# The opening of a hybrid conv/mLSTM block on one Trainium2 core: p in halves of positions, a constant's zeros to warm TensorE, low parts on GpSimd, x loaded and turned in another order

## Chip, core and metric

One core of a Trainium2 chip runs the whole kernel as one launch. The metric is the device time in microseconds (us), as a median over runs. The engines are called by the profile's names: PE is the matrix engine and PEld its weight loads, DVE is VectorE, ACT is ScalarE, POOL is GpSimd, SP is the engine that issues most DMAs. L545 is line 545 of the kernel before.

## The reference, cut to what matters

x is 512 positions by 1024, p is 512 by 256, all in float32.

```python
hn   = rmsnorm(x, g_mix)
proj = hn @ w_in                  # (512, 1024) @ (1024, 14344), split into xa, ba, ..., q, k, v, o, zb, gates
...                               # short convolution, chunked mLSTM, gated merge
x = x + merged @ w_o
gate = sigmoid(rmsnorm(x, g_ple) @ w_ple_gate)
x = x + gate * (p @ w_ple)        # (512, 256) @ (256, 1024): this product is made first, in the opening
return rmsnorm(x, g_final)
```

## The kernel before, in words

Every float32 product is made of three products of a faster format: an operand u is split into a high part `hi` (a copy by ACT that rounds to fp32r) and a low part `lo = u - hi` (a subtraction), and `mm3` (L231 to L235) adds hi·hi, hi·lo and lo·hi into one PSUM bank. Weights come in chunks of 512 rows by 512 columns into four buffers `wraw`; `split_half` (L178) makes the two parts of half a chunk, the high one on ACT (L180) and the low one on DVE, or on POOL if it is told so (L181).

PE, ACT, DVE and POOL run their instructions in the order in which the code states them. SP issues DMAs in the order of the code too; each waits until the transfer that last used one of eight completion semaphores has landed. After the opening the code is a long chain of matmul blocks (plain ones, `block_fm` and `block_tm`, and Strassen products), and the splits of coming weights and the work on results are handed out between the matmul groups by `tick`.

The change lies in the opening, L472 to L640, which does two things before the first block of x @ w_in:

- `ple = p @ w_ple`. p is loaded as `pin` in four tiles of 128 positions (t = 0 to 3), turned by PE into PSUM (`turn_p`, L531, one bank for each half k of the 256 rows), and split into `pT[0]` and `pT[1]`. `w_ple` comes as four quarters (2n + k: n is the half of the 1024 columns, k the half of the 256 rows) into `raws[0]` and is split into `whi[q]` and `wlo[q]`. Each of the eight results (n, t) takes 2 × 3 matmuls of 512 columns; `keep_ple` copies a finished bank out of PSUM, on ACT or, if told so, on DVE (L559), and the copies are stored to DRAM.
- The norm of x. For each tile t: `square_x` on ACT (L535) gives the sum of squares, `power_x` is one small DVE instruction (L538) and a power -0.5 on POOL (L539), `scale_x` is two small DVE instructions (L543, L544) and one over the tile (L545). The first small one needs the power from POOL. `turn_x(k)` (L550) turns column block k of all four tiles and cuts it into `hn_hi` (ACT) and `hn_lo` (DVE) with the gain `gm`, a slice of `prm`, which is `prow` turned by PE (L628) and copied by DVE (L629).

PE's order there: seven matmuls on a zeroed `hn_lo` (`keep_warm`, L491: six at the start, one after the second half of p is turned), the turns of p, the 24 matmuls of n = 0, 21 of the 24 of n = 1, the turn of `prow`, `turn_x(0)` to `turn_x(2)`, the last three matmuls of `ple`, `turn_x(3)`. Then the block on chunk 1 begins, first with the half whose parts `split_half(1, 0)` makes (low part on POOL), and `turn_x(4)` to `turn_x(7)` stand between its groups of six matmuls.

DVE's order for x: `power_x(0)`, a copy of a PSUM bank, `power_x(1)`, the low parts of quarters 2 and 3, `scale_x(0)`, `scale_x(1)`, `power_x(2)`, `power_x(3)`, `scale_x(2)`, `scale_x(3)`, the copy of `prm`, then the low parts of `turn_x`.

POOL's order: small constants, five loads of parameters into `prow` (L512 to L516), the loads of `wg_raw` and `bg` (L517, L518), a memset of `wg` (L526), the four powers, the low parts of chunk 1 (L181).

SP's order: `pin` tiles 0 and 1, quarters 0 and 1 of `w_ple`, x tiles 0 and 1, quarters 2 and 3, x tiles 2 and 3, then the chunks of w_in (L148). ACT issues `pin` tiles 2 and 3.

Of the kernel before, what the change touches and what calls it, by code (L numbers as in the profile page):

```python
# [20 lines left out]
NH = 4  # L21
# [15 lines left out]
def hybrid_block(ctx, tc, x, p, g_mix, w_in, conv_w, conv_b, w_a_out, b_gates, g_head,  # L37
                 w_b_out, w_o, g_ple, w_ple_gate, w_ple, g_final, out):
    nc = tc.nc
    act, dve, pool, pe = nc.scalar, nc.vector, nc.gpsimd, nc.tensor  # L40
# [7 lines left out]
    ps_x = ctx.enter_context(tc.tile_pool(name="ps_x", bufs=4, space=bass.MemoryType.PSUM))  # L48
# [13 lines left out]
    w_in_v = w_in[0].rearrange("(kt p) n -> p kt n", p=P)  # L62
# [6 lines left out]
    chunks, operands = [], []  # L69
    H2 = S // 2  # L70
# [69 lines left out]
    state = {"raw": 0, "split": 0, "use": 0}  # L140
    raws, splits, pieces, active, fresh = {}, {}, deque(), [], []

    def load_raw(between=None):
        i = state["raw"]
        state["raw"] += 1
        raws[i] = spare[i] if i in spare else wraw.tile([P, HC, CW], F32, name=f"wraw{i}", tag="wraw")
        for src, ks, cs in chunks[i]:
            nc.sync.dma_start(raws[i][:, ks, cs], src)  # L148
# [82 lines left out]
    def mm3(ps, a, b, first, last, **kw):  # L231

        pe.matmul(ps, lhsT=a[0], rhs=b[0], start=first, stop=False, **kw)  # L233
        pe.matmul(ps, lhsT=a[0], rhs=b[1], start=False, stop=False, **kw)  # L234
        pe.matmul(ps, lhsT=a[1], rhs=b[0], start=False, stop=last, **kw)  # L235
# [17 lines left out]
    ident = const.tile([P, P], F32, name="ident")  # L253
# [20 lines left out]
    hn_hi = hnp.tile([P, KT, S], F32R, name="hn_hi", align_bytes=256)  # L274
# [14 lines left out]
    def bank(m, tag=None):  # L289
        return ps_mm.tile([P, S], F32, name="mm", tag=tag or order[m // 2], bufs=2)  # L290
# [193 lines left out]
    load_ple(0)

    dve.memset(hn_lo[:, 0, :].bitcast(F32), 0.0)
    warm = bank(2)

    def keep_warm(n):
        for _ in range(n):  # L490
            pe.matmul(warm, lhsT=hn_lo[:, 0, :P], rhs=hn_lo[:, 0, :], start=True, stop=True)  # L491
# [20 lines left out]
    nc.gpsimd.dma_start(prow[0:8, :], g_mix[0].rearrange("(c p) -> c p", p=P))  # L512
# [4 lines left out]
    nc.gpsimd.dma_start(wg_raw, w_in_v[:, :, IG:IG + 2 * NH])  # L517
# [8 lines left out]
    pool.memset(wg.bitcast(F32), 0.0)  # L526

    def turn_p(k):
        pt = bank(k)
        for t in range(NT):  # L530
            pe.transpose(pt[:, t * P:(t + 1) * P], pin[:, t, k * P:(k + 1) * P], ident)  # L531
        return pt

    def square_x(t):
        act.activation(sq, xin[:, t, :], AF.Square, accum_out=ss[:, t:t + 1])  # L535

    def power_x(t):
        dve.tensor_scalar(tmp[0][:, t:t + 1], ss[:, t:t + 1], 1.0 / D, EPS, ALU.mult, ALU.add)  # L538
        pool.tensor_tensor(tmp[1][:, t:t + 1], tmp[0][:, t:t + 1], mhalf[:, :1], ALU.pow)  # L539

    def scale_x(t):
        a, r, e = (u[:, t:t + 1] for u in tmp)
        dve.scalar_tensor_tensor(e, r, a, r, ALU.mult, ALU.mult)  # L543
        dve.tensor_scalar(e, e, -0.5, 1.5, ALU.mult, ALU.add)  # L544
        dve.tensor_scalar(xin[:, t, :], xin[:, t, :], r, e, ALU.mult, ALU.mult)  # L545

    def turn_x(k):
        pt = ps_x.tile([P, S], F32, name="pt", tag="x")
        for t in range(NT):
            pe.transpose(pt[:, t * P:(t + 1) * P], xin[:, t, k * P:(k + 1) * P], ident)  # L550
        cut(hn_hi[:, k, :], hn_lo[:, k, :], pt, gm[:, k:k + 1])
# [4 lines left out]
    def keep_ple(t, n, ps, on_dve=False):  # L556
        u = ples[4 * n + t]
        if on_dve:
            dve.tensor_copy(u, ps)  # L559
        else:  # L560
            act.activation(u, ps, AF.Copy)
# [21 lines left out]
    act.activation(hi, raw, AF.Copy)
# [11 lines left out]
    whi, wlo = ([splits[0][q // HH][u][:, q % HH, :] for q in range(4)] for u in range(2))
    state["use"] = 1
    splits.pop(0)

    def ple_part(ps, n, k, t):
        mm3(ps, [u[:, k, t * P:(t + 1) * P] for u in pT], [whi[2 * n + k], wlo[2 * n + k]], k == 0, k == 1)  # L600

    pss = [ps_x.tile([P, S], F32, name="mmp", tag="x") for t in range(NT)]
    for i, (a, b) in enumerate(((pT[0], whi), (pT[1], whi), (pT[0], wlo))):
        for t in range(NT):
            pe.matmul(pss[t], lhsT=a[:, 0, t * P:(t + 1) * P], rhs=b[0], start=i == 0, stop=False)
# [18 lines left out]
    pss = [bank(t) for t in range(NT)]
    for k, t in [(0, 0), (0, 1), (0, 2), (0, 3), (1, 0), (1, 1), (1, 2)]:
        ple_part(pss[t], 1, k, t)
    pt = ps_x.tile([P, S], F32, name="pt", tag="x")
    pe.transpose(pt[:, :64], prow, ident[:64, :64])  # L628
    dve.tensor_copy(prm, pt[:, :64])  # L629
    for t in range(2):  # L630
        keep_ple(t, 1, pss[t])

    split_half(1, 0, pool)
    for k in range(3):
        turn_x(k)
    ple_part(pss[3], 1, 1, 3)
    for t in range(2, NT):
        keep_ple(t, 1, pss[t])
# [875 lines left out]
```

## Time and profile before

| | |
|---|---|
| median of 3 runs | 838.82 us (838.82 to 839.24) |
| the profiled execution | 839.31 us; its span in the trace 837.2 us |
| PE busy | 826.9 us, 99% of the span, 4520 matmuls |
| DVE, ACT, POOL busy | 680.7, 526.0, 212.8 us |
| DMA | 170.73 MB, mean 204 GB/s |
| granted PE clock | 0.998 on the mean |

A timeline row gives the start in the span, the busy time, the engine, line and operation, what is written and read, and in brackets how long the engine had been idle and for whom it waited. A row of the chain of work gives start, duration and the instruction that was the last thing waited for. Consecutive instructions of one kind are merged into one row (x8).

### The profile page before, as it was taken

The page shows a single profiled execution, that of the slowest core. Times are in us where ns is not written, and L with a number is a line of the kernel's source. Part 1 is how long each engine was busy: PE and PEld are TensorE (multiplying, and loading weights), DVE is VectorE, ACT ScalarE, POOL GpSimd, SP SyncE. Part 2 cuts the span into 40 slices and gives each one's busy share as a digit, 9 for nine tenths or more (in the row PEclk, how much of TensorE's full clock was granted, in tenths as well). Part 3 has the DMA queues.
Part 4 walks back from the last instruction along what each step waited for, and adds up shares of the span by engine and source line. Part 5 has one row for each costly group of instructions (what it writes and reads, how often), then busy time and mean ns, then how long its engine had stood idle before and what let it go on. Part 6 is the DMA issues. An engine that isn't in the chain of part 4 may idle for free.

```text
span 837.2 us, 12110 instructions
## 1 busy us (share of the span) xinstructions
PE 826.9 (99%) x4520; PEld 720.6 (86%) x4520; DVE 680.7 (81%) x938; ACT 526.0 (63%) x778; POOL 212.8 (25%) x213
## 2 busy tenths in 40 slices
PE   9999999999999999999999999999999999999996
PEld 7888888878889988888888999999998888888885
DVE  5788768898888777789978999797985778999565
ACT  7467665788765776667876485545447365657553
POOL 5203122213124221220222334342411212131031
PEclk9999999999999999999999999999999999999999
DMA  9748789759969896985998789999989488999402
GB/s 318 264 150 182 152 220 225 202 182 274 212 149 187 217 240 168 259 215 147 264 225 199 152 179 235 181 182 182 183 268 377 96 191 224 276 260 239 178 1 100
DMA packets 102626, 170.73 MB, mean 204 GB/s; under 512 B 5600, under 2 KB 47124, under 8 KB 101800
## 3 DMA queue, kind: packets, MB, share of 16 engines
q0 software_dynamic: 39136, 69.28, 43.7%
q1 hardware_dynamic: 59792, 94.64, 34.5%
q10 hardware_dynamic: 3640, 6.04, 2.2%
q8 instruction: 35, 0.57, 0.3%
q14 instruction: 23, 0.19, 0.1%
HBM read 153.16 MB, written 16.79 MB: 203 GB/s over the span
## 4 chain that ended last, share of the span: by engine, by line
PE 94%; DVE 2%; DMA 1%; issue 1%; ACT 1%; POOL 0%; POOLq 0%; ACTq 0%
PE mm L233 29%; PE mm L234 29%; PE mm L235 29%; DMA wraw<-in_w_in 1%; PE pv L235 1%; PE pv L233 1%; PE pv L234 1%; PE sc L235 1%; PE sc L234 1%; PE sc L233 1%; PE ptk L1307 0%; PE pth L1188 0%; PE pt L550 0%; PE mm L491 0%; DVE xin L545 0%
## 5 line engine op out<-in xcount | busy, mean ns | idle before, releaser
L181 DVE TENSOR_TENSOR wlo<-wraw,whi 128x1024 fp32r<-128x1024 f32 x244 | 299.5, 1228 | 83.0 <-ACT whi L180 76.3
L180 ACT ACTIVATE whi<-wraw 128x1024 fp32r<-128x1024 f32 x246 | 257.9, 1054 | 85.4 <-PE mm L235 36.1
L156 POOL DMA_DIRECT2D wraw<-in_w_in x106 | 129.3, 1395 | 294.7 <-DVE wlo L181 200.1
L346 ACT ACTIVATE s<-mm 128x512 f32<-128x512 f32 x84 | 50.2, 598 | 83.4 <-PE mm L235 82.2
L233 PE MATMUL mm<-whi,hs 128*128 128x512 f32 x256 | 99.8, 390 | 0.4 <-DVE c L350 0.4
L234 PE MATMUL mm<-wlo,hs 128*128 128x512 f32 x256 | 99.9, 390 | 0.2 <-DVE wlo L181 0.2
L235 PE MATMUL mm<-whi,hs 128*128 128x512 f32 x256 | 99.7, 389 | 0.0
L233 PE MATMUL mm<-hn_hi,whi 128*128 128x256 f32 (+1 forms) x304 | 93.3, 307 | 0.0
L235 PE MATMUL mm<-hn_hi,wlo 128*128 128x256 f32 (+1 forms) x304 | 93.1, 306 | 0.0
L234 PE MATMUL mm<-hn_lo,whi 128*128 128x256 f32 (+1 forms) x304 | 92.9, 305 | 0.0
L233 PE MATMUL mm<-hs,whi 128*128 128x256 f32 x320 | 90.6, 283 | 0.0
L234 PE MATMUL mm<-hs,whi 128*128 128x256 f32 x320 | 90.6, 283 | 0.0
L235 PE MATMUL mm<-hs,wlo 128*128 128x256 f32 x320 | 90.6, 283 | 0.0
L233 PE MATMUL mm<-whi,hn_hi 128*128 128x512 f32 x192 | 74.7, 389 | 0.0
L234 PE MATMUL mm<-wlo,hn_hi 128*128 128x512 f32 x192 | 74.7, 389 | 0.0
L235 PE MATMUL mm<-whi,hn_lo 128*128 128x512 f32 x192 | 74.7, 389 | 0.0
L233 PEld LDWEIGHTS mm<-hs,whi 128*128 128x128 f32 x320 | 61.4, 192 | 0.0
L234 PEld LDWEIGHTS mm<-hs,whi 128*128 128x128 f32 x320 | 61.4, 192 | 0.0
L235 PEld LDWEIGHTS mm<-hs,wlo 128*128 128x128 f32 x320 | 61.4, 192 | 0.0
L235 PEld LDWEIGHTS mm<-hn_hi,wlo 128*128 128x128 f32 x304 | 58.1, 191 | 2.9 <-POOL wlo L181 0.3
L234 PEld LDWEIGHTS mm<-hn_lo,whi 128*128 128x128 f32 x304 | 58.1, 191 | 2.4
L233 PEld LDWEIGHTS mm<-hn_hi,whi 128*128 128x128 f32 x304 | 58.1, 191 | 2.4
(345 smaller groups left out, 1728.1 us busy)
## 6 DMA issues: line engine op xcount, KB each, us to landing
wraw<-in_w_in SPq DMA_DIRECT2D x32, 1024.0 KB, 5.3
wraw<-in_w_in SPq DMA_DIRECT2D x48, 512.0 KB, 4.9
wraw<-in_w_in POOLq DMA_DIRECT2D x46, 512.0 KB, 7.6
wraw<-in_w_in POOLq DMA_DIRECT2D x60, 256.0 KB, 5.8
wraw<-in_w_b_out SPq DMA_DIRECT2D x7, 1024.0 KB, 6.9
wraw<-in_w_b_out POOLq DMA_DIRECT2D x12, 512.0 KB, 6.8
wraw<-in_w_o SPq DMA_DIRECT2D x5, 1024.0 KB, 6.9
wraw<-in_w_a_out SPq DMA_DIRECT2D x4, 1024.0 KB, 5.1
```

The costliest lines, as they stand in the source:

```text
L156: nc.gpsimd.dma_start(raws[to][:, ks, cs], src[:, ks, :], accum_op=ALU.add)
L180: act.activation(hi, t, AF.Copy)
L181: (e_lo or dve).tensor_tensor(lo, t, hi.bitcast(F32), ALU.subtract)
L233: pe.matmul(ps, lhsT=a[0], rhs=b[0], start=first, stop=False, **kw)
L234: pe.matmul(ps, lhsT=a[0], rhs=b[1], start=False, stop=False, **kw)
L235: pe.matmul(ps, lhsT=a[1], rhs=b[0], start=False, stop=last, **kw)
L346: act.activation(to[i], src, AF.Copy, scale=scale)
```

## The change

- Loads. Quarter 0 of `w_ple` goes first, on ACT's queue. SP then takes `pin` tiles 0 and 1, `pin` tiles 2 and 3, quarter 1, x tiles 0 and 1, quarter 2, x tiles 2 and 3, quarter 3. Each chunk-1 load is cut in two (256 KB pieces, both column pieces of the first 256 rows before those of the second).
- PE is warmed by eight matmuls of 128 columns on a constant's zeros; the memset of `hn_lo` and the seventh warming matmul are gone.
- p is turned, copied and split in halves of positions (256 columns of a bank at a time); the first matmuls run on tiles 0 and 1 while tiles 2 and 3 are still to be turned.
- The low parts of all four quarters of `w_ple` are subtracted by POOL. The high part of quarter 3 is made by DVE. `wg`'s memset moves to the front of POOL's loads, and the loads of `wg_raw` and `bg` behind the low parts of quarters 0 and 1.
- x is turned by halves: tiles 0 and 1 for column blocks 0 to 3, then tiles 2 and 3. `power_x(3)` stands behind `scale_x(2)` and the copy of `prm`, and the low part of quarter 3 (POOL) between that power and `scale_x(3)`.

```diff
     qk_block(1)
+    chunks[1] = [(src[:, k:k + HH], slice(k, k + HH), cs) for k in (0, HH) for src, _, cs in chunks[1]]
     qk_block(0)
...
-    for i, queue in enumerate((nc.sync, nc.scalar)):
-        queue.dma_start(pin[:, 2 * i:2 * i + 2, :], p_v[:, 2 * i:2 * i + 2, :])
-    def load_ple(n):
-        for src, ks, cs in chunks[0][2 * n:2 * n + 2]:
-            nc.sync.dma_start(raws[0][:, ks, cs], src)
-    load_ple(0)
-    dve.memset(hn_lo[:, 0, :].bitcast(F32), 0.0)
+    def load_ple(q, queue=nc.sync):
+        src, ks, cs = chunks[0][q]
+        queue.dma_start(raws[0][:, ks, cs], src)
+    load_ple(0, nc.scalar)
+    for i in range(2):
+        nc.sync.dma_start(pin[:, 2 * i:2 * i + 2, :], p_v[:, 2 * i:2 * i + 2, :])
+    load_ple(1)
     warm = bank(2)
-    def keep_warm(n):
-        for _ in range(n):
-            pe.matmul(warm, lhsT=hn_lo[:, 0, :P], rhs=hn_lo[:, 0, :], start=True, stop=True)
-    keep_warm(6)
+    zeros = nc.const_aps.tensor(0.0, [P, P], F32)
+    for _ in range(8):
+        pe.matmul(warm[:, :P], lhsT=zeros, rhs=zeros, start=True, stop=True)
...
-    for i in range(2):
-        for t in range(2 * i, 2 * i + 2):
-            nc.sync.dma_start(xin[:, t, :], x_v[:, t, :])
-        if i == 0:
-            load_ple(1)
+    for t in range(NT):
+        nc.sync.dma_start(xin[:, t, :], x_v[:, t, :])
+        if t % 2:
+            load_ple(2 + t // 2)
     load_raw()
+    pool.memset(wg.bitcast(F32), 0.0)
...
-    nc.gpsimd.dma_start(wg_raw, w_in_v[:, :, IG:IG + 2 * NH])
-    nc.gpsimd.dma_start(bg, b_gates[0].rearrange("(g h) -> h g", g=2))
-    pool.memset(wg.bitcast(F32), 0.0)
...
-    ptp = turn_p(0)
-    dve.tensor_copy(pT[0][:, 0, :], ptp)
...
-    low(pT[0][:, 0, :], pT[1][:, 0, :], ptp)
-    low(hi, lo, raw)
-    ptp = turn_p(1)
-    keep_warm(1)
-    split_quarter(1, dve)
-    cut(pT[0][:, 1, :], pT[1][:, 1, :], ptp)
...
-    power_x(0)
-    keep_ple(0, 0, pss[0], True)
-    power_x(1)
-    for hi, lo, raw in quarters:
-        act.activation(hi, raw, AF.Copy)
-        low(hi, lo, raw)
-    keep_ple(1, 0, pss[1])
-    scale_x(0)
-    scale_x(1)
-    for t in (2, 3):
-        square_x(t)
-        power_x(t)
-    scale_x(2)
-    scale_x(3)
...
+    for k in range(2):
+        turn_p(k, first)              # first, second = (0, 1), (2, 3): tiles of positions
+    turn_p(0, second)
+    high(0)                           # high: ACT copy of a quarter
+    for ts in (first, second):
+        c = slice(ts[0] * P, (ts[-1] + 1) * P)
+        dve.tensor_copy(pT[0][:, 0, c], ptp[0][:, c])
+        low(pT[0][:, 0, c], pT[1][:, 0, c], ptp[0][:, c])
+    low(*quarters[0], pool)
+    ple_pass(0, 0, 0, first)          # ple_pass(n, k, part, tiles): one matmul for each tile
+    turn_p(1, second)
+    ple_pass(0, 0, 1, first)
+    for i in range(2):
+        ple_pass(0, 0, i, second)
+    ple_pass(0, 0, 2, range(NT))
+    high(1)
+    cut(pT[0][:, 1, :], pT[1][:, 1, :], ptp[1])
+    low(*quarters[1], pool)
+    nc.gpsimd.dma_start(wg_raw, w_in_v[:, :, IG:IG + 2 * NH])
+    nc.gpsimd.dma_start(bg, b_gates[0].rearrange("(g h) -> h g", g=2))
+    for t in range(NT):
+        ple_tile(0, 1, t)             # the three matmuls of one tile
     for t in range(2):
         square_x(t)
+    high(2)
     power_x(0)
+    scale_x(0)
     power_x(1)
+    low(*quarters[2], pool)
+    keep_ple(0, 0, pss[0, 0])
+    keep_ple(1, 0, pss[0, 1], True)
     scale_x(1)
+    square_x(2)
+    power_x(2)
+    keep_ple(3, 0, pss[0, 3])
+    keep_ple(2, 0, pss[0, 2], True)
+    square_x(3)
+    pss.update({(1, t): bank(t) for t in range(NT)})
+    for i in range(3):
+        ple_pass(1, 0, i, range(NT))
+    pts = [turn_x(k, first) for k in range(HC)]
+    pe.transpose(pts[3][:, H2:H2 + 64], prow, ident[:64, :64])
+    dve.tensor_copy(whi[3], quarters[3][2])
     scale_x(2)
+    dve.tensor_copy(prm, pts[3][:, H2:H2 + 64])
+    power_x(3)
+    low(*quarters[3], pool)
     scale_x(3)
...
+    for i in range(3):
+        ple_pass(1, 1, i, first)
     split_half(1, 0, pool)
+    for t in first:
+        keep_ple(t, 1, pss[1, t])
+    for k in range(HC):
+        turn_x(k, second, pts[k])
+    for t in second:
+        ple_tile(1, 1, t)
+        keep_ple(t, 1, pss[1, t])
     split_half(1, 1, pool)
```

The four banks of `turn_x` are those that the results (0, t) leave: bank k is free once `keep_ple` of tile k has read it.

More of the change, by code (lines that the diff above doesn't have):

```diff
@@ L525, in hybrid_block, with turn_p @@
     gp = prm[:, 56:64]
[L526 to L532, printed above, removed]
+    ptp = [bank(k) for k in range(2)]
+    def turn_p(k, ts):
+        for t in ts:
+            pe.transpose(ptp[k][:, t * P:(t + 1) * P], pin[:, t, k * P:(k + 1) * P], ident)
     def square_x(t):
@@ L545, in scale_x, with turn_x @@
         dve.tensor_scalar(xin[:, t, :], xin[:, t, :], r, e, ALU.mult, ALU.mult)
-    def turn_x(k):
-        pt = ps_x.tile([P, S], F32, name="pt", tag="x")
-        for t in range(NT):
+    def turn_x(k, ts=range(NT), pt=None):
+        pt = pt or ps_x.tile([P, S], F32, name="pt", tag="x")
+        for t in ts:
             pe.transpose(pt[:, t * P:(t + 1) * P], xin[:, t, k * P:(k + 1) * P], ident)
-        cut(hn_hi[:, k, :], hn_lo[:, k, :], pt, gm[:, k:k + 1])
+        if ts[-1] == NT - 1:
+            cut(hn_hi[:, k, :], hn_lo[:, k, :], pt, gm[:, k:k + 1])
+        return pt
     def join_x(k):
@@ L565, in hybrid_block @@
         split_tiles(0, h)
-    def split_quarter(q, e_lo):
-        hi, lo = (u[:, q % HH, :] for u in splits[0][q // HH])
-        raw = raws[0][:, q, :]
-        act.activation(hi, raw, AF.Copy)
-        e_lo.tensor_tensor(lo, raw, hi.bitcast(F32), ALU.subtract)
     def quarter(q):
@@ L575, in quarter, with high @@
         return hi, lo, raws[0][:, q, :]
-    def low(hi, lo, src):
-        dve.tensor_tensor(lo, src, hi.bitcast(F32), ALU.subtract)
-    ptp = turn_p(0)
-    dve.tensor_copy(pT[0][:, 0, :], ptp)
-    hi, lo, raw = quarter(0)
-    act.activation(hi, raw, AF.Copy)
-    low(pT[0][:, 0, :], pT[1][:, 0, :], ptp)
-    low(hi, lo, raw)
-    ptp = turn_p(1)
-    keep_warm(1)
-    split_quarter(1, dve)
-    cut(pT[0][:, 1, :], pT[1][:, 1, :], ptp)
+    def high(q):
+        hi, _, raw = quarters[q]
+        act.activation(hi, raw, AF.Copy)
@@ new lines, in low, with ple_pass @@
+    def low(hi, lo, src, e=dve):
+        e.tensor_tensor(lo, src, hi.bitcast(F32), ALU.subtract)
+    quarters = [quarter(q) for q in range(4)]
+    whi, wlo = ([u[i] for u in quarters] for i in range(2))
+    splits.pop(0)
+    state["split"] = 2
+    state["use"] = 1
+    del raws[0]
+    pss = {(n, t): ps_x.tile([P, S], F32, name="mmp", tag="x") if n == 0 else None for n in range(2) for t in range(NT)}
+    PART = [(0, 0), (1, 0), (0, 1)]
+    def ple_pass(n, k, i, ts):
+        u, v = PART[i]
+        for t in ts:
+            pe.matmul(pss[n, t], lhsT=pT[u][:, k, t * P:(t + 1) * P], rhs=(whi, wlo)[v][2 * n + k],
+                      start=(k, i) == (0, 0), stop=(k, i) == (1, 2))
@@ new lines, in ple_tile @@
+    def ple_tile(n, k, t):
+        for i in range(3):
+            ple_pass(n, k, i, (t,))
+    first, second = (0, 1), (2, 3)
+    for k in range(2):
[10 more added lines that the diff above has]
+    ple_pass(0, 0, 1, first)
@@ L590, in hybrid_block @@
+    for i in range(2):
[8 more added lines that the diff above has]
+        ple_tile(0, 1, t)
     for t in range(2):
         square_x(t)
-    quarters = [quarter(q) for q in (2, 3)]
-    state["split"] = 2
-    del raws[0]
@@ L595, in hybrid_block @@
[L595 to L605, printed above, removed]
@@ L606, in hybrid_block @@
-    for t in range(NT):
-        ple_part(pss[t], 0, 1, t)
+    high(2)
     power_x(0)
-    keep_ple(0, 0, pss[0], True)
+    scale_x(0)
     power_x(1)
-    for hi, lo, raw in quarters:
-        act.activation(hi, raw, AF.Copy)
-        low(hi, lo, raw)
-    keep_ple(1, 0, pss[1])
-    scale_x(0)
-    scale_x(1)
-    for t in (2, 3):
-        square_x(t)
-        power_x(t)
+    low(*quarters[2], pool)
+    keep_ple(0, 0, pss[0, 0])
+    keep_ple(1, 0, pss[0, 1], True)
+    scale_x(1)
+    square_x(2)
@@ L620, in hybrid_block @@
+    power_x(2)
[8 more added lines that the diff above has]
+    dve.tensor_copy(whi[3], quarters[3][2])
     scale_x(2)
+    dve.tensor_copy(prm, pts[3][:, H2:H2 + 64])
+    power_x(3)
+    low(*quarters[3], pool)
     scale_x(3)
-    for t in (2, 3):
-        keep_ple(t, 0, pss[t])
@@ L624, in hybrid_block @@
[L624 to L631, printed above, removed]
-    split_half(1, 0, pool)
[L634 to L638, printed above, removed]
@@ L639, in hybrid_block @@
-    turn_x(3)
+    for i in range(3):
+        ple_pass(1, 1, i, first)
+    split_half(1, 0, pool)
+    for t in first:
[5 more added lines that the diff above has]
+        keep_ple(t, 1, pss[1, t])
     split_half(1, 1, pool)
```

## Prediction

> **What bounds the kernel now.** I read the page first, then the busy time before and after the first matmul on hn, then the chain of work through that point, then the timelines of the four engines in the opening.
>
> ```profile
> PE 826.9 (99%) x4520; PEld 720.6 (86%) x4520; DVE 680.7 (81%) x938; ACT 526.0 (63%) x778; POOL 212.8 (25%) x213
> ```
> ```profile
> 0.00:20.06 20.06, 18.53 (x80) 14.72 (x80) 11.64 (x29) 13.87 (x23) 10.91 (x22) 1.00 0.94 317
> 20.06:837.20 817.14, 808.36 (x4443) 705.84 (x4441) 669.03 (x910) 512.11 (x756) 201.88 (x192) 1.00 0.80 201
> ```
>
> From 20 us on PE is busy 808.36 of 817.14 us: the rest of the kernel is one queue of matmuls, and it moves with the moment at which the first matmul on hn starts. The change edits only what lies before that moment, so the question is when the new opening hands over. The chain through the hand-over:
>
> ```profile
> 13.97 0.81 DVE xin L545
> 14.78 0.08 DVE rtmp L538
> ...
> 14.93 0.56 POOL rtmp L539
> ...
> 15.96 0.81 DVE xin L545
> ...
> 17.13 0.82 DVE xin L545
> ...
> 17.99 1.20 PE pt L550 x9
> ...
> 19.89 0.44 PE pt L550 x4
> 20.33 0.23 PE mm L233
> ```
>
> The opening ends not on matmuls but on DVE: scale of x tile 1, square sum and power of tile 2, scale of tiles 2 and 3 (done at 17.95), and then PE's turns and three matmuls of `ple` (17.99 to 20.09, 2.1 us). PE's 18.53 busy us in the opening mislead: what decides is when the last `scale_x` ends.
>
> Does a shift reach the end? The one later place where PE waits long is this:
>
> ```profile
> 153.53 0.24 PE mm L235
> ...
> 157.39 9.27 DMA wraw<-in_w_in
> ...
> 167.83 1.24 DVE wlo L181
> ...
> 170.97 0.51 PE mm L233
> ```
>
> That load is started by work that follows PE's own matmul at 153.53, so it moves with PE. I carry the shift to the end one for one.
>
> **The change part by part.** Rows that price it, from ACT, POOL, DVE, PE and SP:
>
> ```profile
> 5.42 0.63 ACT L583 ACTIVATE whi<-wraw 128x512 fp32r<-128x512 f32 x1 [2.87 <-DMA wraw<-in_w_ple]
> ...
> 8.01 1.06 ACT L535 ACTIVATE hnf<-xin 128x1024 f32<-128x1024 f32 x1 [0.83 <-DMA xin<-in_x]
> ...
> 9.45 1.06 ACT L535 ACTIVATE hnf<-xin 128x1024 f32<-128x1024 f32 x1 [0.29 <-DMA xin<-in_x]
> 10.41 0.19 ACT L535 ACTIVATION_READ_ACCUMULATOR hnf<-xin 128x1 f32 x1
> ...
> 11.55 0.57 ACT L561 ACTIVATE ple<-mmp 128x512 f32<-128x512 f32 x1
> 12.66 1.06 ACT L535 ACTIVATE hnf<-xin 128x1024 f32<-128x1024 f32 x1 [0.54 <-DMA xin<-in_x]
> ...
> 13.97 1.06 ACT L535 ACTIVATE hnf<-xin 128x1024 f32<-128x1024 f32 x1 [0.15 <-DMA xin<-in_x]
> ...
> 1.81 0.76 POOL L512 DMA_DIRECT2D prow<-in_g_mix  x1
> ...
> 4.66 0.97 POOL L517 DMA_DIRECT2D wg_raw<-in_w_in  x1
> ...
> 6.23 0.97 POOL L526 MEMSET wg<- 128x1024 f32 x1
> 9.50 0.57 POOL L539 TENSOR_TENSOR rtmp<-rtmp,mhalf 128x1 f32<-128x1 f32 x1 [2.30 <-DVE rtmp L538]
> ...
> 22.78 2.43 POOL L181 TENSOR_TENSOR wlo<-wraw,whi 128x1024 fp32r<-128x1024 f32 x1 [2.15 <-ACT whi L180]
> ...
> 806.48 1.31 POOL L1396 TENSOR_TENSOR xg<-xr,gfin 128x512 f32<-128x512 f32 x1 [4.51 <-DVE xr L1387]
> ...
> 10.49 0.69 DVE L559 COPY ple<-mmp 128x512 f32<-128x512 f32 x1 [1.15 <-PE mmp L235]
> ...
> 12.37 0.21 DVE L543 SCALAR_TENSOR_TENSOR rtmp<-rtmp,rtmp 128x1 f32<-128x1 f32 x1
> 12.61 0.15 DVE L544 TENSOR_SCALAR rtmp<-rtmp 128x1 f32<-128x1 f32 x1
> ...
> 15.15 0.15 DVE L538 TENSOR_SCALAR rtmp<-ss 128x1 f32<-128x1 f32 x1 [0.30 <-ACT hnf L535]
> ...
> 17.85 0.22 DVE L629 COPY prm<-pt 128x64 f32<-128x64 f32 x1
> ...
> 22.67 0.19 DVE L645 TENSOR_TENSOR wg<-wg_raw,wg 128x32 fp32r<-128x32 f32 x1
> ...
> 22.99 2.27 DVE L645 TENSOR_TENSOR wg<-wg_raw,wg 128x32 fp32r<-128x32 f32 x1
> ...
> 821.73 0.49 DVE L1450 TENSOR_SCALAR y<-xg,fs 128x512 f32<-128x512 f32 x1
> ...
> 1.48 2.93 PE L491 MATMUL mm<-hn_lo 128*128 128x512 f32 x6 [1.48 <-DVE hn_lo L486]
> 4.39 1.94 PE L531 MATMUL mm<-ident,pin 128*128 128x128 f32 x8
> ...
> 20.09 0.48 PE L233 MATMUL mm<-hn_hi,whi 128*128 128x512 f32 x1
> ...
> 5.67 12.60 SPq L148 DMA_DIRECT2D wraw<-in_w_in  x8
> ```
>
> *Warming and p by halves.* Six zero matmuls (to 4.39) waited for p, not p for them. No row shows a plain float32 product of zeros; the nearest, turns of 128 columns, took 1.94 / 8 = 0.24 us, so eight take about 1.9 us; at the price of a 512-column warming matmul each (2.93 / 6 = 0.49) they would end about 0.3 us after p's landing if they start at 0.8, which n = 0 has room for. Zero cost, covered by the load of p. The first half of p is issued by SP as before, so the turns start near 4.4 again; the second half now stands second on SP, where quarter 0 stood, so it lands about when quarter 0 did (ACT's row at 5.42: 5.4). Against that goes one 0.49 us warming matmul, and the first products need half the copies. I put the 24 matmuls of n = 0 at 12.3, as before, with 11.3 to 14 as bounds; none of it is on the path below.
>
> *Loads.* The transfers stand in one queue. x tiles 0 and 1 have the same bytes ahead of them as before (8.0 and 9.4, the starts of their squares). Tile 2 loses 256 KB of `w_ple` ahead of it and tile 3 too, some 0.8 us each at the 317 GB/s of the opening's row, so 11.8 and 13.1 by their squares' rows, quarter 3 about 13.9. ACT squares tile 2 only after `high(2)` (0.63) and one copy (0.57): 9.45 + 1.15 + 0.63 + 0.57 = 11.8 to 13.1; tile 3, after another copy, 13.7 to 15.0. These gains end in front of DVE, which takes them later. Chunk 1 in four pieces costs SP two issues more, with nothing waiting behind; its first half lands about 1.5 us before the whole. The loads of a later chunk (in SP's row to 18.27) wait for `raws[0]`, which POOL now frees at about 20.0; PE needs it three blocks later (three times 48 matmuls of 0.23 us, past 50 us). Zero.
>
> *POOL.* `wg`'s memset (0.97) goes ahead of the five `prow` issues (4.66 - 1.81 = 2.85): done at 1.81 + 0.97 + 2.85 = 5.65. A low part of 128x512 has the row of 1.31 us (half of 2.43 would be 1.2). Quarters 0 and 1: to 7.0 and 8.3, both before PE needs them. Then `wg_raw` and `bg` (6.23 - 4.66 = 1.57) to 9.9. `power_x(0)` is ready for POOL at 9.6 and waits for that: 9.9 to 10.5.
>
> *DVE, the path.* It loses four subtractions but gains one PSUM copy (0.69 each, two in place of one) and the high part of quarter 3 (no row; between 0.49, a pass in SBUF over as many elements, and 0.69; I take 0.49, since it reads SBUF). A scale is 0.21 + 0.15 + 0.81 with hops, 1.24 (12.37 to 13.61).
> - `scale_x(0)` 10.5 to 11.75; square 1's small step to 11.95; copy (1,0) to 12.65; POOL's power 1 to 12.6.
> - Right behind power 1 POOL starts the low part of quarter 2: 12.6 to 13.9. L543 of `scale_x(1)` comes up at 12.65. It reads two tensors in SBUF, as L645 does: 0.19 us alone, 2.27 us when POOL's subtraction of 22.78 had begun, ending at 25.26 with it. So I hold L543 until 13.95; `scale_x(1)` ends at 15.0, where before it ended at 14.78.
> - Small step 15.15; copy (2,0) 15.85; high part 16.35; `scale_x(2)` 17.6 (before: 16.77); `prm` 17.85; only then the small step of tile 3, 18.05 (before: 15.3); power 3 on POOL 18.1 to 18.65; low part of quarter 3 to 19.97; L543 of `scale_x(3)` held to 20.0, L545 done at 21.05.
>
> [...]
>
> *PE behind it.* Column blocks 0 to 3 of tiles 0 and 1 are turned early, about 15.0 to 16.4; bank 2 waits for copy (2,0). The products with quarter 3's low part wait on POOL until 20.0, so PE idles some 2.5 us from 17.4. After 21.05: eight turns (twice 0.44) and six matmuls (1.38), 2.25 us, and the first matmul on hn at 23.3, where the row before has 20.09. Small gaps of 0.1 in the first group go. **Sum:** 21.05 - 17.95 = 3.1, plus 2.25 - 2.1 = 0.15, less 0.15: **+3.1 us**.
>
> The sum stands against the profiled execution, 839.31 us (span 837.2), which is 0.49 above the median of the runs; 838.82 + 3.1 = **841.9 us**. About 0.2%, 1.7 us, is what a measurement of this kernel can tell from no change.
>
> **The rivals.**
>
> *POOL does not hold DVE.* L543 comes up within 0.1 us of POOL's start at both places, and a DVE instruction that is first keeps its turn (the first L645 at 22.67 ran 0.19 us). If L543 slips in and L545 runs beside POOL, `scale_x(1)` ends at 13.9, the small step of tile 3 at 16.95, `scale_x(3)` at 18.9, but the low part of quarter 3 still ends at 19.0 and PE passes it first, then needs ACT's cuts behind two copies: +1.9, 840.7 us. If L545 is held although L543 slipped in: about 20.5, +2.7, 841.5 us, which I count with the forecast.
>
> *The earlier x decides: not slower.* If DVE's copies and POOL's low parts find earlier places than I give them, the path is again from the last tile of x to its scale. Before, from square 3's start 13.97 to 17.95 it took 4.0 us; with tile 3 at 13.1 and no wait that is 17.1, PE's 2.25 us behind it: 19.35, -0.75, 838.1 us. For it speaks that tiles 2 and 3 waited for their loads (0.54 and 0.15 idle on ACT); against it, that DVE's order itself puts copy, high part, scale 2, `prm` and a POOL power before `scale_x(3)`. It decides only if DVE is done with `scale_x(1)` by 12.5, which power 1 at 12.6 excludes unless POOL is free over 1 us earlier. Together with a part of the waits between 153 and 171 us it would be faster by over 0.2%.
>
> *The clock of PE comes later.* The new warming is other work; if it is not enough, matmuls of n = 0 take 0.49 instead of 0.23 us for some us more. n = 0 ends at 14, `prm`'s turn is late, and scale 3 by 0.45: 842.3 us. Something like it would also come from a longer load at 157 us.
>
> **How the numbers follow.** Forecast (POOL holds DVE, +2.7 to +3.2) 0.48; no hold, +1.9 (mostly beyond 1.7 us) 0.18; later still (842.3 to 843) 0.08; a remainder between -1.7 and +1.7, the earlier x among it, 0.18; faster by more 0.08. Slower: 0.48 + 0.11 + 0.08 = 0.67; same: 0.07 + 0.18 = 0.25; faster 0.08. The likeliest alone: 841.2 to 842.4. The range takes in no hold and a part of the remainder: 839.2 to 843.0 us.
>
> **What would show it.** In the new timeline: `wg_raw` issued about 8.3 and the first power about 9.9; the POOL subtractions of 1.3 us right behind the second and the fourth power; L543's successor 1.2 us long or late there; DVE's copy of `prm` ahead of the last small step, and that step near 18.0; an idle PE between 17.4 and 20; the first matmul on hn at 23.3. The prediction is wrong if the last scale ends before 18 us, if POOL's low parts take well under 1.3 us, or if the shift at 20 us does not stand at 830 us.

## The result, and the profile after

The changed kernel takes 844.35 us (median of 6 runs, 844.08 to 845.81) where the kernel before, timed beside it, takes 839.03 (6 runs, 838.35 to 839.85): the ratio is 1.0063, 95% interval 1.0053 to 1.0073. It is slower, as forecast, but by 5.3 us and not by 3.1, and the time lies 1.35 us above the range. The profiled execution took 844.16 us with a span of 842.4. Line numbers from here on are those of the changed kernel: L538 to L540 are `scale_x` (L543 to L545 before), L533 and L534 `power_x`, L545 the turns of x, L573 a low part of a quarter, L182 a low part of chunk 1, L588 the products of `ple`, L234 to L236 the block's matmuls.

Busy time by engine, from the page:

```profile
PE 829.1 (98%) x4529; PEld 722.9 (86%) x4529; DVE 680.7 (81%) x937; ACT 524.9 (62%) x776; POOL 217.3 (26%) x217
```

The same by stretches (start:end, length, busy time of PE, PEld, DVE, ACT and POOL with instructions, granted PE clock, DMA share, GB/s), cut where the clock changes and where the first matmul on hn starts:

```profile
0.00:19.06 19.06, 15.80 (x74) 13.07 (x75) 10.21 (x25) 9.97 (x16) 13.91 (x26) 1.00 0.93 309
19.06:25.89 6.83, 5.29 (x17) 4.00 (x17) 5.47 (x8) 4.11 (x7) 2.11 (x1) 0.50 1.10 363
25.89:842.00 816.11, 808.00 (x4441) 705.86 (x4439) 665.04 (x906) 510.79 (x753) 201.28 (x191) 1.00 0.80 199
```

The last row answers to the row of 808.36 busy us before: the same work, 808.00 us of it. The opening now lasts 25.9 us instead of 20.1, and in its last 6.83 us the clock of PE is at 0.50; before, it is that low only from 833.25 us on, with no matmul left. (Ahead of the clock's first rise, at 5.41 us here and 7.22 before, the trace has no record of the clock, and the column reads 1.00 there.) The chain of work through the hand-over (start, duration, what was waited for):

```profile
12.37 1.26 DVE rtmp L538
...
17.09 0.55 POOL rtmp L534
...
17.66 1.22 DVE rtmp L538
...
18.91 0.17 DVE rtmp L539
...
19.10 2.63 DVE xin L540
...
21.77 1.75 PE pt L545 x7
23.53 2.53 PE mm L588 x6
26.06 0.24 PE mm L234
```

It is the chain that was forecast, with two pieces of another size: the pass over tile 3 took 2.63 us (0.82 before), and PE's turns and six products 1.75 + 2.53 = 4.28. Which instructions stood beside them is in the timeline; POOL:

```profile
12.31 1.29 POOL L573 TENSOR_TENSOR wlo<-wraw,whi 128x512 fp32r<-128x512 f32 x1
...
17.60 1.26 POOL L573 TENSOR_TENSOR wlo<-wraw,whi 128x512 fp32r<-128x512 f32 x1
18.82 2.35 POOL L182 TENSOR_TENSOR wlo<-wraw,whi 128x1024 fp32r<-128x1024 f32 x1
```

DVE:

```profile
12.37 1.25 DVE L538 SCALAR_TENSOR_TENSOR rtmp<-rtmp,rtmp 128x1 f32<-128x1 f32 x1
...
13.84 0.81 DVE L540 TENSOR_SCALAR xin<-xin,rtmp,rtmp 128x1024 f32<-128x1024 f32 x1
...
17.66 1.21 DVE L538 SCALAR_TENSOR_TENSOR rtmp<-rtmp,rtmp 128x1 f32<-128x1 f32 x1 [0.66 <-POOL rtmp L534]
...
19.10 2.62 DVE L540 TENSOR_SCALAR xin<-xin,rtmp,rtmp 128x1024 f32<-128x1024 f32 x1
```

Read ends, not starts. L538 ends at 13.62 and 18.87, POOL's subtractions of the quarters at 13.60 and 18.86: the one-element instruction (128x1, one element in each partition) ends with POOL, 0.01 to 0.02 us behind it. The pass ends at 21.72; POOL's subtraction for chunk 1, `split_half(1, 0)`, at 21.17, so the pass had 0.55 us of its 0.81 left to do when POOL was done. Chunk 1's subtraction was ready to go and stood in POOL's queue right behind quarter 3's. L538 held DVE until that queue had moved on to it, so the pass met it.

PE:

```profile
18.91 1.11 PE L588 MATMUL mm<-wlo,pT 128*128 128x512 f32 x2 [1.43 <-POOL wlo L573]
19.82 0.42 PE L545 MATMUL pt<-ident,xin 128*128 128x128 f32 x1
21.77 1.75 PE L545 MATMUL pt<-ident,xin 128*128 128x128 f32 x7 [1.54 <-DVE xin L540]
...
25.89 0.41 PE L234 MATMUL mm<-hn_hi,whi 128*128 128x512 f32 x1
```

PE waits twice, for quarter 3's low part and for tile 3's scale; after the first wait the clock halves. The seven turns then take 1.75 us, 0.25 each, where the rows of before have 0.11 from turn to turn (x12 in 1.80 with a wait in it, x4 in 0.44 in the chain).

### The profile page after: what moved, and what is told of

Read it like the earlier page. It is cut to its first block, busy times and chain, and to the rows that moved or that the text cites. A ratio compares the mean times of both kernels' runs of the same rounds, so it can differ in the third digit from the quotient of the medians.

```text
span 842.4 us, 12131 instructions
## 1 busy us (share of the span) xinstructions
PE 829.1 (98%) x4529; PEld 722.9 (86%) x4529; DVE 680.7 (81%) x937; ACT 524.9 (62%) x776; POOL 217.3 (26%) x217
## 4 chain that ended last, share of the span: by engine, by line
PE 93%; DVE 2%; DMA 2%; issue 1%; ACT 1%; POOL 1%; SPq 0%; POOLq 0%; ACTq 0%
PE mm L234 29%; PE mm L236 28%; PE mm L235 28%; PE pv L236 1%; PE pv L235 1%; PE pv L234 1%; DMA wraw<-in_w_in 1%; PE sc L236 1%; PE sc L235 1%; PE sc L234 1%; DMA wraw<-in_w_ple 1%; PE pt L545 0%; PE ptk L1321 0%; PE pth L1202 0%; DVE xin L540 0%
## 5 line engine op out<-in xcount | busy, mean ns | idle before, releaser
L182 DVE TENSOR_TENSOR wlo<-wraw,whi 128x1024 fp32r<-128x1024 f32 x244 | 299.5, 1228 | 83.6 <-ACT whi L181 77.5
L234 PE MATMUL mm<-whi,hs 128*128 128x512 f32 x256 | 99.9, 390 | 0.4 <-ACT yc L835 0.4
L236 PE MATMUL mm<-whi,hs 128*128 128x512 f32 x256 | 99.7, 389 | 0.0
L234 PE MATMUL mm<-hn_hi,whi 128*128 128x256 f32 (+1 forms) x304 | 93.2, 307 | 0.0
L236 PE MATMUL mm<-hn_hi,wlo 128*128 128x256 f32 (+1 forms) x304 | 93.0, 306 | 0.0
L234 PE MATMUL mm<-hs,whi 128*128 128x256 f32 x320 | 90.6, 283 | 0.0
L236 PE MATMUL mm<-hs,wlo 128*128 128x256 f32 x320 | 90.6, 283 | 0.0
L234 PE MATMUL mm<-whi,hn_hi 128*128 128x512 f32 x192 | 74.7, 389 | 0.0
L236 PE MATMUL mm<-whi,hn_lo 128*128 128x512 f32 x192 | 74.7, 389 | 0.0
L234 PEld LDWEIGHTS mm<-hs,whi 128*128 128x128 f32 x320 | 61.4, 192 | 0.0
L236 PEld LDWEIGHTS mm<-hs,wlo 128*128 128x128 f32 x320 | 61.4, 192 | 0.0
L234 PEld LDWEIGHTS mm<-hn_hi,whi 128*128 128x128 f32 x304 | 58.2, 192 | 2.5
L236 PEld LDWEIGHTS mm<-hn_hi,wlo 128*128 128x128 f32 x304 | 58.1, 191 | 2.6
```

The costliest lines, as they stand in the source:

```text
L182: (e_lo or dve).tensor_tensor(lo, t, hi.bitcast(F32), ALU.subtract)
```

## The experiments

Theory at the outset: POOL's subtractions hold DVE's scales (the small two-input instruction and then the pass), and the clock that falls behind PE's waits costs the rest. Rivals: that DVE is late because of its new order or the later loads, hold or no hold; that the fall of the clock alone is the cause.

**One input instead of two.** The changed kernel, with one line of `scale_x` rewritten: the operand that is a column of 128 values goes in as the instruction's scalar.

```diff
-        dve.scalar_tensor_tensor(e, r, a, r, ALU.mult, ALU.mult)
+        dve.tensor_scalar(e, r, a, r, ALU.mult, ALU.mult)
```

> Hold theory: DVE's small instruction of a scale waits for POOL only because it reads two tensors in SBUF. With one tensor and two per-partition scalars it takes about 0.22 us instead of 1.25 (tile 1) and 1.21 (tile 3); the pass over tile 3 then comes up inside POOL's 1.26 us subtraction instead of inside the 2.35 us one, and ends near 19.4 instead of 21.7. That takes 2.3 us off, 842.0 us, and up to 1.9 more (840.1) if PE's shorter idle time keeps its clock. Rival (the order of DVE's work is the cause, not POOL): the last scale still ends late and the time stays at 844.3.

839.34 us (10 runs; ratio to before 1.0004, interval 0.9995 to 1.0014). The time is back at that of the kernel before, 0.8 us below the lowest figure expected. DVE's timeline:

```profile
12.52 0.27 DVE L538 TENSOR_SCALAR rtmp<-rtmp,rtmp 128x1 f32<-128x1 f32 x1
...
13.02 1.28 DVE L540 TENSOR_SCALAR xin<-xin,rtmp,rtmp 128x1024 f32<-128x1024 f32 x1
...
17.39 0.27 DVE L538 TENSOR_SCALAR rtmp<-rtmp,rtmp 128x1 f32<-128x1 f32 x1 [0.66 <-POOL rtmp L534]
...
17.89 1.25 DVE L540 TENSOR_SCALAR xin<-xin,rtmp,rtmp 128x1024 f32<-128x1024 f32 x1
```

and POOL's:

```profile
17.32 1.26 POOL L573 TENSOR_TENSOR wlo<-wraw,whi 128x512 fp32r<-128x512 f32 x1
18.54 2.84 POOL L182 TENSOR_TENSOR wlo<-wraw,whi 128x1024 fp32r<-128x1024 f32 x1
```

L538 runs beside POOL in 0.27 us. The pass over tile 3 now comes up while POOL is still at quarter 3, ends 0.56 us behind that (18.58 and 19.14), and POOL's next subtraction is the one that waits: 2.84 us instead of 2.35. Last scale 2.58 us earlier, clock kept at full speed (1.00), first matmul on hn at 21.47. In hn's start this one line is 4.42 us: 2.58 in the scale and 1.84 in PE's work behind it. That start is still 1.38 us later than before (20.09); the spans are equal even so because PE, in these two profiles, loses 1.2 us to a load near 170 us in the kernel before and nothing here (last point of the next section).

The control, the same line in the kernel before:

> The kernel before, with the small instruction of scale_x that reads two SBUF tensors written with one. There POOL subtracts nothing until 22.8 us, when the last scale has been done for 5 us, and the instruction took 0.21 us. The hold theory: no change, 838.5 to 839.7 us, all four small instructions near 0.2 to 0.27 us. The rival, that the one-input form is worth something by itself (and so that what it gave in the changed kernel was not the hold): faster by 1 us or more, below 838.

839.23 us beside 839.47 (ratio 0.9997, interval 0.9987 to 1.0007); the four small instructions took 0.27 us each. So the one-input form is worth nothing by itself; what it gave above was the hold.

**Chunk 1's low part back on DVE.**

```diff
-    split_half(1, 0, pool)
+    split_half(1, 0)
```

> The low part of the first half of chunk 1 goes from POOL (2.35 us) to DVE (1.23 us, behind the last scale). Hold theory: the pass over tile 3 takes 0.81 instead of 2.62 us, the last scale ends at 19.9, the time falls by 1.8 to 842.5; with the clock kept also, to 840.6. The two-input small instruction is still held by the subtraction of quarter 3. Rival (the pass over a tile does not share anything with POOL and was late for another reason): unchanged, or up to 1.2 us slower for the work put on DVE.

841.27 us (10 runs; 1.0021, 1.0012 to 1.003). Chain of waits at the same place:

```profile
19.12 0.82 DVE xin L540
```

L538 of tile 3 is still held (1.21 us from 17.68), the pass no longer, and the clock stays up (1.00). The prediction's working had no hold of this pass and no fall of the clock, as it is here, and put the loss at 3.1 us: 1.9 are measured (841.27 less 839.35), with the first matmul on hn at 22.18, 2.1 us later than before. PE's work behind the last scale takes 2.25 us here (19.93 to 22.18), just what the prediction gave it.

**The four quarters' low parts back on DVE, chunk 1's left on POOL.**

```diff
-    low(*quarters[q], pool)     # each of the four
+    low(*quarters[q])
```

> The changed kernel with the low parts of the four quarters of w_ple back on DVE (0.68 us each), the low part of chunk 1 still on POOL. Hold theory: what matters is which POOL subtraction stands beside the scales. The small instruction of tile 1 takes 0.22 us again, but POOL starts chunk 1's low part near 16.7 and now holds the low part of quarter 3 on DVE until 19.1; the last scale ends near 21 and PE's clock falls in its wait: 842.5 to 844.5, hardly better. Rival (the quarters' low parts on POOL are the loss themselves): 5 us back, 839.3.

844.43 us (4 runs; 1.0061, 1.0046 to 1.0076). Nothing is gained by taking away POOL's four small subtractions: the one of chunk 1 then starts right behind the fourth power, when L538 comes up. POOL and DVE:

```profile
19.71 2.34 POOL L182 TENSOR_TENSOR wlo<-wraw,whi 128x1024 fp32r<-128x1024 f32 x1
```

```profile
19.77 2.29 DVE L538 SCALAR_TENSOR_TENSOR rtmp<-rtmp,rtmp 128x1 f32<-128x1 f32 x1 [0.44 <-POOL rtmp L534]
```

Again the ends agree, 22.05 and 22.06. In this profile the clock fell too (below), so the time holds both.

**No subtraction on POOL in the opening**, the last two edits together:

> As the last one, with the low part of chunk 1's first half on DVE too, so that POOL subtracts nothing beside the scales. Hold theory: nothing is held, the two-input small instructions take 0.22 us, the last scale ends near 19.1, the clock stays, the first matmul on hn starts near 21.4: 839 to 840, as with the one-input form, although DVE has 4 us more of work. Rival (DVE's load is the bound and POOL a relief): slower than the changed kernel, 845 or more.

840.0 us (10 runs; 1.0011, 1.0001 to 1.002). L538 0.22 and the pass 0.81 us everywhere; the last scale ends at 20.85 all the same: DVE now makes the subtractions itself (0.68 us each), and in this profile, whose clock came up late, at 10.03, it also waits 0.92 us for PE's turn of `prow`. The first matmul on hn comes at 23.12.

**The fourth power early**, ahead of quarter 3's high part; quarter 3's subtraction on POOL stays behind `prm`'s copy in the code, but no longer waits for the power:

```diff
+    power_x(3)
     dve.tensor_copy(whi[3], quarters[3][2])
     scale_x(2)
     dve.tensor_copy(prm, pts[3][:, H2:H2 + 64])
-    power_x(3)
     low(*quarters[3], pool)
```

> The changed kernel with the power of tile 3 ahead of the high part of quarter 3 and of scale 2, as the kernel before has it. Rival theory (DVE's order, the late power, is the loss): the last scale ends 2 us earlier and the time falls to 841 or less. Hold theory: the power moves POOL's subtractions forward, scale 2 is held by the one of quarter 3 and scale 3 by the one of chunk 1, so the last scale still ends near 21 and the time is 843 to 844.5.

842.56 us (4 runs; 1.0045, 1.003 to 1.006). The hold moves to other instructions: the pass over tile 2 takes 1.85 us beside quarter 3's subtraction, L538 of tile 3 2.17 beside chunk 1's. DVE and POOL:

```profile
16.12 1.85 DVE L540 TENSOR_SCALAR xin<-xin,rtmp,rtmp 128x1024 f32<-128x1024 f32 x1
...
18.03 2.17 DVE L538 SCALAR_TENSOR_TENSOR rtmp<-rtmp,rtmp 128x1 f32<-128x1 f32 x1
```

```profile
16.14 1.28 POOL L573 TENSOR_TENSOR wlo<-wraw,whi 128x512 fp32r<-128x512 f32 x1
17.39 2.79 POOL L182 TENSOR_TENSOR wlo<-wraw,whi 128x1024 fp32r<-128x1024 f32 x1
```

The pass over tile 2 started 0.02 us ahead of POOL's subtraction and was held all the same. The last scale ends at 21.23, as the hold expects, and PE waits 2.93 us for it, up to 21.29; the time is 0.4 us below the range given, and in the profile the clock did not fall (1.00). Being ready earlier is worth 0.5 us in the scale while POOL's queue holds it.

**The clock: filling PE's waits.** Products of zeros, added into a bank that is being summed, stand where PE waited (7 before the products with quarter 3's low part, 9 before the turns of tiles 2 and 3); the holds stay.

```diff
+    def fill(n):
+        for _ in range(n):
+            pe.matmul(pss[1, 2][:, :P], lhsT=zeros, rhs=zeros, start=False, stop=False, ...)
     for i in range(3):
+        if i == 2:
+            fill(7)
         ple_pass(1, 1, i, first)
+    fill(9)
```

> Seven and nine products of zeros, added to a bank in use, fill PE's two waits. Clock theory: the granted clock stays full, eight turns and six matmuls behind the last scale take 2.25 us instead of 4.1, and the time falls by 1.9 to about 842.4, with the last scale still at 21.7. Rival (the clock falls for another reason, or the wait is all there is): 844.3.

843.01 us (4 runs; 1.0038, 1.0023 to 1.0053). PE:

```profile
21.63 1.27 PE L545 MATMUL pt<-ident,xin 128*128 128x128 f32 x8
...
24.12 0.40 PE L234 MATMUL mm<-hn_hi,whi 128*128 128x512 f32 x1
```

The clock stays up (1.00), the first matmul on hn is at 24.12 instead of 25.89, the time 1.3 us lower. The last scale is as late as it was (21.85 for 21.72), but PE's work behind it takes 2.27 us and not 4.17. So the fall is worth 1.3 to 1.8 us, and the hold, with its scales and waits, the rest. The rival that the fall alone is the cause falls with it.

**Is the fall certain?** Second profiles of the changed kernel and of the one with the early power:

> The changed kernel as it is, a second profile for the clock. If its waits set the clock off every time: the granted clock falls to 0.5 again near 19 us and stays there for about 6.8 us, the first matmul on hn is at 25.5 to 26.3, the time 844 to 845. If the fall hangs on where a counter of the chip's own stands: the clock stays at full speed in this profile or falls elsewhere, and the first matmul on hn comes at 23.9 to 24.6.

> The kernel with the fourth power early, a second profile for the clock: in the first, PE waited 3.1 us and the clock did not fall. If a wait of some length sets the clock off: no fall again, first matmul on hn at 23.3 to 23.7, 842 to 842.9 us. If the fall hangs on a counter of its own: falls in this profile, first matmul on hn at 24.8 to 25.6, 843.4 to 844.5 us.

844.68 and 842.68 us; the clock fell again in the first and not in the second, but neither was a copy of its first profile: the clock rose later, and the first matmul on hn came at 26.83 and 25.43, behind both ranges given. The mean granted clock of whole runs speaks for a fall each time: in the changed kernel's six runs it is 0.992 to 0.995, in 24 of the kernel before 0.996 to 0.998 and in ten of the one-input version 0.997 to 0.998; 3.41 us at half clock lower this mean by 0.002. In the second profile of the changed kernel it rose at 10.28 (5.41 in the first) and fell at 23.93, for 3.41 us only. The trace gives these times on a raster: from rise to fall 13.65 us in both profiles, and in the one of the quarters' low parts on DVE, four times 3.41, and the fall lasts two or one times 3.41. Cut along this raster, the stretches ahead of a fall, and the emptiest ones without a fall, are these. The changed kernel, first profile (the clock falls at 19.06 and rises at 25.89):

```profile
15.65:19.06 3.41, 1.98 (x11) 1.22 (x10) 2.64 (x7) 0.98 (x1) 1.98 (x3) 1.00 1.10 348
19.06:22.48 3.42, 1.88 (x7) 1.18 (x8) 2.62 (x2) 1.28 (x3) 2.11 (x1) 0.50 1.10 358
22.48:25.89 3.41, 3.41 (x12) 2.83 (x11) 2.85 (x6) 2.83 (x5) 0.00 (x0) 0.50 1.09 369
```

Its second profile (fall at 23.93):

```profile
20.52:23.93 3.41, 1.38 (x9) 0.99 (x10) 2.68 (x2) 1.36 (x3) 2.16 (x1) 1.00 1.09 369
```

The quarters' low parts on DVE (fall at 24.02):

```profile
20.60:24.01 3.41, 0.85 (x8) 0.85 (x9) 2.43 (x3) 0.89 (x2) 1.45 (x1) 1.00 1.09 369
```

The power early, first profile (no fall):

```profile
16.11:19.52 3.41, 2.25 (x11) 1.31 (x9) 3.40 (x3) 1.27 (x3) 3.41 (x3) 1.00 1.10 349
19.52:22.94 3.42, 1.65 (x11) 1.52 (x12) 2.20 (x4) 1.28 (x3) 0.66 (x1) 1.00 1.10 348
```

One wait of 2.93 us lies across two stretches there, and no fall follows. In the three profiles with a fall the clock changed only at edges of this raster, and where the edges lie in the kernel differs from run to run (the rise at 5.41 and 10.28 in the two of the changed kernel). What a fall hangs on isn't settled: PE's busy time doesn't order the cases (1.65 us without a fall, 1.98 with one), the time of weight loads does (0.85, 0.99 and 1.22 ahead of the three falls; 1.31 at the least without one, over the openings of all profiles here, from the rise of the clock on), which is agreement in a handful of stretches and no proof.

**The new order of loads alone**, in the kernel before (quarter 0 on ACT's queue; quarter 1, x tiles 0 and 1, quarter 2, x tiles 2 and 3, quarter 3; chunk 1 in halves):

```diff
-    load_ple(0)
+    load_ple(0, nc.scalar)
...
+    load_ple(1)
...
+    for t in range(NT):
+        nc.sync.dma_start(xin[:, t, :], x_v[:, t, :])
+        if t % 2:
+            load_ple(2 + t // 2)
```

> The kernel before with the new order of loads alone (quarter 0 first on ACT's queue, p on SP, x tiles 2 and 3 ahead of quarter 3, chunk 1 in four pieces). If the last tile of x bounds the opening: tiles 2 and 3 land 1.2 us earlier and the time falls by up to 1.0, to 838.0. If DVE's order bounds it (the chain of before names DVE ahead of each scale): within 0.4 of 839.0.

841.14 us (9 runs; 1.0026, 1.0014 to 1.0038), where 839.4 at most was expected. The timelines of ACT and DVE say why:

```profile
14.08 0.63 ACT L613 ACTIVATE whi<-wraw 128x512 fp32r<-128x512 f32 x1 [2.78 <-DMA wraw<-in_w_ple]
14.62 0.58 ACT L562 ACTIVATE ple<-mmp 128x512 f32<-128x512 f32 x1
15.10 1.05 ACT L536 ACTIVATE hnf<-xin 128x1024 f32<-128x1024 f32 x1
```

```profile
14.74 0.69 DVE L579 TENSOR_TENSOR wlo<-wraw,whi 128x512 fp32r<-128x512 f32 x1 [1.04 <-ACT whi L613]
15.35 0.21 DVE L544 SCALAR_TENSOR_TENSOR rtmp<-rtmp,rtmp 128x1 f32<-128x1 f32 x1
```

Quarter 3 is now the last to land, and the old code has its high part on ACT ahead of the square of tile 2 and its low part on DVE ahead of the first scale. DVE's is the delay that counts: the first scale starts at 15.35 instead of 12.37, 2.98 us later, and the last one ends at 20.92 instead of 17.94, as much later. The square of tile 2 starts at 15.10 instead of 12.66, but DVE takes its sum only at 17.69, behind the scale of tile 1. The changed kernel doesn't have this fault: quarter 3's high part is made by DVE and its low part by POOL, and the scales of tiles 0 to 2 stand ahead of that low part; there tile 2 is squared at 11.57 and tile 3 at 13.09. The expectation erred because it looked at the landing of x and not at what stood ahead of it on ACT and DVE.

**What the best order gives.** One-input form, the fourth power early and ahead of both scales, the pass over tile 3 on ACT instead of DVE, two copies of `ple` on DVE instead of ACT:

```diff
+        if t == 3:
+            act.activation(xin[:, t, :], xin[:, t, :], AF.Copy, scale=e)
...
-        keep_ple(t, 1, pss[1, t])
+        keep_ple(t, 1, pss[1, t], True)
```

> A version that follows from the hold theory: one-input small instructions, the power of tile 3 early, the pass over tile 3 on ACT (1.06 us, nothing shared with POOL), the copies of (0,1) and (1,1) on DVE. Scale 2 is held once by quarter 3's low part and ends near 17.4, scale 3 on ACT near 17.7, the first matmul on hn starts near 20.0: 837 to 838.5. If PE's own work from its first product at 6.6 is the bound instead, no better than 838.5; if ACT's pass is held as well, 840 or more.

839.05 us (10 runs; 1.0005, 0.9992 to 1.0018), not the 837 to 838.5 expected: 5 us better than the changed kernel, equal to the one before. First matmul on hn at 20.36. What is left is PE itself:

```profile
6.39 0.70 PE L602 MATMUL mmp<-whi,pT 128*128 128x512 f32 x2 [0.61 <-DVE pT L616]
...
18.15 0.98 PE L559 MATMUL pt<-ident,xin 128*128 128x128 f32 x7 [0.29 <-ACT xin L552]
...
20.36 0.40 PE L234 MATMUL mm<-hn_hi,whi 128*128 128x512 f32 x1
```

From the first product on it waits only 0.29 us. None of these versions beats the kernel before: with this work in the opening, PE is full from 6.4 us to the hand-over at 20.4.

## Why the prediction was off

The sum put the first matmul on hn at 23.3; it came at 25.89. The 2.6 us between are the last scale (21.05 predicted, 21.72 measured: +0.67) and PE's work behind it (2.25 predicted, 4.17 from 21.72 to 25.89: +1.9).

- *What bounds: right.* The last `scale_x` decides, and the kernel behind the hand-over takes as long as it did (808.36 and 808.00 busy us).
- *Warming: right.* The products of zeros end at 4.52, ahead of the first turn of p at 4.97, which waits for p (4.4 had been predicted). There are sixteen in the trace for the eight in the code, 0.23 us each.
- *p by halves: right at nothing.* First product at 6.64 (6.56 before), the last of n = 0 begins at 12.17 (12.11 before). DVE's copy of the first half, at 6.06, started only when all six turns in its bank and the next were done.
- *Loads, POOL: right.* The squares of tiles 2 and 3 came at 11.57 and 13.09, 0.2 and 0.6 us earlier than their ranges; `wg_raw` at 8.21 (8.3), the first power at 9.75 (9.9), the low parts 1.26 to 1.29 (1.31). (POOL's sum to 5.65 should read 5.63; 5.57 is measured.)
- *L538 held by POOL's low parts: right, at both places.* 12.37 to 13.62 for the predicted 12.65 to 13.95; 17.66 to 18.87 for the predicted end at 20.0. The second is 1.1 us earlier because instructions that were laid end to end overlap on DVE by 0.07 to 0.1 each, because tile 1 was done 0.35 earlier, and because the high part took 0.42 and not 0.49. The rival without a hold falls with this, and so does the one of the earlier x, which needed DVE to be done with `scale_x(1)` by 12.5: it ended at 14.65.
- *The pass over tile 3: the step that failed.* It was costed at its 0.81 us alone. The prediction named a subtraction of chunk 1 on POOL (its second half, the row of 2.43) as what held an instruction at 22.99 in the kernel before, and took it as a row to price with, but did not ask where the one of the first half would go: behind quarter 3's in POOL's queue, just when the pass comes up. It cost 1.81 us and ate the 1.1 us of the point above.
- *PE behind the scale: the second that failed.* Its idle time from 17.4 was predicted ("some 2.5 us from 17.4") and given no price; the clock was a rival for the warming alone, at +0.45. The filled waits put the fall at 1.3 to 1.8 us; with the clock up, the work took the 2.25 us of the sum (2.25 and 2.27 in two versions).
- *The shift carried one for one: within a microsecond and a half.* hn's start moved by 5.8 us, the span by 5.2. With the one-input form it moved by 1.38 and the time by nothing: the waits that PE has between 150 and 200 us aren't fixed. Before, after, and with one input, by stretches:

```profile
150.00:200.00 50.00, 49.41 (x217) 40.28 (x216) 45.05 (x55) 39.99 (x63) 11.77 (x16) 1.00 0.70 196
```

```profile
150.00:200.00 50.00, 49.58 (x218) 40.45 (x217) 44.41 (x53) 38.79 (x62) 8.80 (x13) 1.00 0.70 199
```

```profile
150.00:200.00 50.00, 50.00 (x222) 41.39 (x222) 45.91 (x57) 41.15 (x65) 12.40 (x17) 1.00 0.73 206
```

  With one input PE doesn't wait there at all. Counted along the sequence of matmuls from the first on hn, it is 1.22 us behind the kernel before at the 661st (167.96 and 166.74) and 0.04 us behind at the 701st (177.03 and 176.99). The wait belongs to the load that the prediction took to move with PE. POOL issues it at 157.39 before and at 158.59 with one input, and ACT, which waits for it, starts at 166.74 and 166.64. Before, then with one input:

```profile
166.74 1.06 ACT L180 ACTIVATE whi<-wraw 128x1024 fp32r<-128x1024 f32 x1 [2.79 <-DMA wraw<-in_w_in]
```

```profile
158.59 1.19 POOL L157 DMA_DIRECT2D wraw<-in_w_in  x1 [1.24 <-DVE wlo L182]
...
166.64 1.06 ACT L181 ACTIVATE whi<-wraw 128x1024 fp32r<-128x1024 f32 x1 [1.48 <-DMA wraw<-in_w_in]
```

  So the issue moved with PE, but the load itself was 1.3 us shorter: from issue to the start on ACT 8.05 us instead of 9.35. This is luck for the one-input version, not its merit, and what sets the length of the load is open.

The range was too narrow at the top: it took the hold of the pass only where L543 slips in first, and a late clock only behind the warming. The two terms added to the forecast, 841.9 + 0.67 + 1.9, give 844.5.

No row of before shows POOL holding a pass over a tile, and the prediction's +2.7, for a pass that is held although L543 slipped in, rests on none: it was an assumption of the author's. The runs show the hold of the pass: 2.62 us in the changed kernel, 1.85 with the early power, 1.28 and 1.25 with one input, for a pass of 0.81, each ending 0.55 to 0.56 us behind POOL's instruction.

## What to carry to other kernels

Before a subtraction is given to POOL, follow POOL's queue past that instruction, and lay each of its entries beside the DVE instructions that come up at that time: here both the small ones with two SBUF inputs (up to 2.29 us for 0.21) and the passes over a tile (up to 2.62 us for 0.81) were held until POOL was done. A one-element instruction that took its second operand as a scalar was not held (0.27 us), and that one line was worth 5 us. A wait of PE can cost more than its length (the fall of the clock was worth 1.3 to 1.8 us): after stretches of 3.41 us with 0.85 to 1.98 us of PE work the clock was at half speed for one or two more stretches in three profiles, while in another it stayed up after 1.65 us. Price both cases and let the range hold them, since the stretches' edges move from run to run.

## What had not been expected of the hardware

- One SBUF input alone doesn't tell what is held. The one-element DVE instruction with two SBUF inputs (0.21 us) took 1.25, 1.21, 2.29 and 2.17 us beside POOL's subtractions and ended with them, as forecast; the same arithmetic with one SBUF input and scalars took 0.27 beside them, but a pass over 1024 elements with one SBUF input and scalars was held (up to 2.62 us for 0.81).
- The hold worked both ways and in turns: where a DVE instruction was waiting as one POOL subtraction ended, POOL's next was the one to wait (2.84 and 2.79 us instead of 2.35). Being first didn't help the pass: it came up 0.02 and 0.03 us ahead of POOL's subtraction in the two profiles with the early power and was held.
- PE's clock rose between 3.67 and 12.11 us after the start over the 13 profiles, at 5.41 and 10.28 in the two of the changed kernel; in the opening it fell in three of them, 13.65 us or four times 3.41 behind the rise, after stretches in which PE was busy for 25 to 58% of the time.
- A plain float32 product of 128 columns is two instructions in the trace; on zeros at the start, 0.23 us each.
